# Recurrence's columns ahead of attention's values, and one stream for cached keys and values

## The chip, the cores and the metric

The kernel runs on one core of one Trainium2 chip. The metric is the time on the device of one execution in microseconds (us), the median of three runs. TensorE (PE) multiplies matrices, VectorE (DVE), ScalarE (ACT) and GpSimd (POOL) do the rest, and 16 DMA engines move data between HBM and the on-chip memory. POOL issues the gathers of cached pages, SyncE (SP) all other transfers.

## What is computed

Two decoder layers for a prompt of 256 tokens and 8 samples of one token each, which have 2048 cached positions in pages of 128. All 264 rows go through the same weights. Cut to what matters here, layer 0:

```python
x = x + 0.5 * swiglu(rms_norm(x), w_gate, w_up, w_down)         # FFN 0
qkv, z, b, a, dq, dk, dv = jnp.split(rms_norm(x) @ w_in, ...)   # the mixer's input projection
gq, gk, gv = split(silu(causal_conv(qkv)))                      # the recurrence's queries, keys, values
o_g, S = gdn_chunked(l2norm(gq), l2norm(gk), gv, g, beta, S0)   # samples: gdn_recurrent, one step
o_g = rms_norm(o_g, g_norm) * silu(z)
k, v = gather_pages(cache_diff_k, page_table), gather_pages(cache_diff_v, page_table)   # samples only
o_d = diff_attend(dq, pos, [(k, v, ...), (dk, dv, pos)], lam, ...)   # softmax over the past and the new token
x = x + concat([o_g, o_d]) @ w_out                              # then FFN 1
```

Layer 1 is FFN 2, a latent attention with its own cache (ckv, kpe), and FFN 3; a final norm follows. Everything is float32.

## The kernel before

**Order of work.** The kernel is written as threads (Python generators). A planner, class Clock, estimates when each instruction could start and puts the instructions of all threads into the engines' queues in that order; `urgent` threads have a bonus (gdn and gdn_s 80, proj 0; line 1759), `flow` threads may run ahead. Each queue is then fixed and runs in order on the chip. Where PE would be idle by the plan, it gets matmuls of a constant (tile ps_pe, line 666). Nearly every instruction is issued through line 457, so rows are told apart by their tiles.

**Weights.** Class Stream loads units of 16 blocks of 128 x 128 (1 MB, tile raw), splits them by fours into a high and a low part (ACT and DVE, tile whl), and each block makes three matmuls of 264 columns. `W.limit` stops it at the end of the input projection until post_g calls `W.resume`.

**The mixer of layer 0** (from line 1143). proj (1162) computes the columns of WIN (line 118), 128 features each, eight blocks a column: dq, dk, dv (attention's queries, keys, values), gk, gq, gv (the recurrence's; each goes through a convolution on DVE, ACT and POOL), z. At gk0 it waits for the scores of sample 1 (1169), since tile S2, where the recurrence's columns go, serves as three key slots before. The other threads: dpv (1582) makes the samples' query weights and, after dv3, the token-major values ("vtok"); diff_p (1617) the prompt's attention, after vtok; diff_s (1659) the samples' scores, one sample after the other, by scores (1023); diff_v (1680) weighs their values, by weigh (1057), after vtok; gdn (1266) the recurrence over the prompt, after gk3, gq3 and, in its second half, gv3; gdn_s (1457) its step for the samples, after the last column; post_g (1716) and post_d (1730) the norms and the two halves of the output projection (tile mix).

**The caches.** Class Loader (970) gathers tiles in order into whichever slots are free; a slot is given back when its tile has been used, but not a slot that is a piece of another tile (ya, yb, S2). LK loads keys: per sample 8 tiles of 128 x 1024 (0.5 MB). LV loads values: per sample 4 tiles of 128 x 2048 (1 MB), one for each strip. LK has 4 pieces of ya and yb, 8 own slots (N_DK) and 3 pieces of S2; LV has 2 slots (N_DV). FFN 0 hands them out one by one (`side`). After proj LK gets four whl slots, which it must give back before post_g ("dk retired"); after gdn_s LV gets xh and xl. PE_ has two pairs of score buffers, so scores of sample b wait until sample b - 2 is weighed (1671). Layer 1 has loaders mk (8 slots of 0.65 MB) and mv.

```python
LK = Loader("dk", 1024, [(kpool, ptk[:, i, 4 * b + g:4 * b + g + 1]) for b in range(NS) for i in range(2) for g in range(4)], [])
LV = Loader("dv", 2048, [(vpool, pt[:, 4 * (NS + b) + g:4 * (NS + b) + g + 1]) for b in range(NS) for g in range(4)], [])
```

Of the kernel before, what the change touches and what calls it, by code (L numbers as in the profile page):

```python
# [37 lines left out]
N_DK, N_DV = 8, 2  # L38
N_MK, N_MV = 8, 2
# [78 lines left out]
WIN = [n + str(h) for n in ("dq", "dk", "dv", "gk", "gq", "gv", "z") for h in range(4)]  # L118
# [24 lines left out]
class Virtual:  # L143
    """A tile whose place is chosen when its first instruction is put into a queue."""
# [5 lines left out]
class Slots:  # L150
    """Places of one shape for virtual tiles. The place of a tile is free again when its thread has gone past the
    segment that made it (keep: when the thread has called free) and its last instruction is in a queue."""
# [35 lines left out]
class Clock:  # L188
    """Puts the instructions that the threads create into the engine queues in the order of their
    estimated starts, so that no queue waits long at its head."""  # L190
# [16 lines left out]
    # -- tiles  # L207
# [48 lines left out]
    def when(self, r, write, eng=None):  # L256
        """When an instruction of `eng` may use the region."""
# [32 lines left out]
    # -- cost estimates  # L290
# [47 lines left out]
    # -- instructions  # L338
# [91 lines left out]
    def pe(self, t, c, cols, share):  # L430
        """The tensor engine's clock is halved in each tick after one in which few columns left the array."""
        if self.columns.get(int(t // self.TICK) - 1, 0.0) < self.FULL:
            c *= 2.0
        k = int((t + c) // self.TICK)
        self.columns[k] = self.columns.get(k, 0.0) + cols * share
        return t + c

    def keep_warm(self, t):
        """Matmuls that nobody reads, up to time t."""
# [52 lines left out]
    def add(self, name):  # L492
        """What the current thread has created so far makes `name` available."""
        if not self.cur:
            self.done[name] = 0.0
        else:
            self.cur.marks.append((name, self.seq))
            self.settle(self.cur)

    # -- threads: generators that yield None (go on when all that they issued is done), a time, or the  # L500
    # names they wait for
# [53 lines left out]
def hybrid_trunk_kernel(ctx: ExitStack, tc: tile.TileContext, wall, xT, wba, vecs, cst0, cst1, ident_d, convst,  # L555
# [29 lines left out]
    def service(thread, f, *a):  # L585
        """f's instructions in a thread of their own, which nobody waits for as a whole."""
# [5 lines left out]
    # ------------------------------------------------------------ weight stream  # L592
    class Stream:
        """The weights, 128 x 128 blocks in the order of their use; units of 16 blocks are loaded, pieces of 4 split into
        a high and a low part, except those that raw() hands out whole."""
# [54 lines left out]
        def whole(self, use):  # L650
            """use(the next block); with float32 products for these there is nothing to split."""
# [13 lines left out]
    # in the tensor engine's gaps it multiplies a constant, so that its clock stays up  # L665
# [17 lines left out]
    def rsqrt(src, w, np_=128):  # L683
        """1/sqrt of a small tile on the vector engine."""
# [17 lines left out]
    # ------------------------------------------------------------ constants  # L702
# [30 lines left out]
    # ------------------------------------------------------------ norm statistics  # L733
# [19 lines left out]
    def norm_rows(n, squares, scale, eps):  # L753
        """squares: n tiles [128, NT]. For tile i, rows 32 i and 32 i + 1 of the result add up to
        1 / sqrt(scale * (sum over the partitions) + eps)."""
# [32 lines left out]
    class Rstd:  # L788
        """The thread that computes mul / sqrt(scale * sum of acc over the partitions + eps), for every row; get()
        yields it to a thread that needs it."""  # L790
# [31 lines left out]
    # ------------------------------------------------------------ driver  # L822
    def run(*threads):
        loaders = [LK.thread, LV.thread]
# [5 lines left out]
    def flow(gen, bonus=0.0):  # L830
        """A thread that goes on as soon as its matrix products are in the queue."""
        return gen, True, bonus

    def urgent(gen, bonus=BONUS):
        """A thread whose instructions go first even if others could start a little earlier."""
# [8 lines left out]
    def lead(xh, xl, tags):  # L844
        """The first blocks of a projection; the last rows of x come latest, so the first two blocks alternate."""
# [17 lines left out]
    # ------------------------------------------------------------ FFN  # L863
# [58 lines left out]
    # ------------------------------------------------------------ final norm  # L922
# [18 lines left out]
    def finish_y():  # L941
        """The statistics with the tokens on the partitions; a product with their diagonal spreads them."""
# [21 lines left out]
    # ------------------------------------------------------------ KV gather  # L964
# [3 lines left out]
    ptk = sb.tile([128, 2, 4 * NS], I32, name="ptk")  # L968

    class Loader:  # L970
        """Gathers tiles of 32-row strips of four pages each, in order, into whichever slots are free."""
# [40 lines left out]
        def retire(self, tags):  # L1012
            """These slots are not filled again."""
# [8 lines left out]
    # ------------------------------------------------------------ one sample's softmax over its past  # L1022
    def scores(b, w, load, parts, SM, ready, cc, P, pT):
        """w [128, sub, 32]: the queries, one diagonal block for each page of a strip; parts: for each part
        of the features, its four strips' tiles. Leaves exponentials (strip, page, query row; key) in P,
        transposed in pT; returns the inverses of their sums."""
# [25 lines left out]
        r = small("tr", 1)  # L1052
# [1161 lines left out]
```

## Time and profile before

| | before |
|---|---|
| median of 3 runs | 1344.3 us (1342.5 to 1350.9) |
| span of the profiled execution, first to last instruction | 1297.2 us |
| median less span: what lies around it | 47.1 us |
| PE busy | 1274.9 us, 98% |
| PE weight load, DVE, ACT, POOL busy | 88%, 67%, 45%, 33% |
| DMA | 287.7 MB, mean 222 GB/s |
| mean granted clock of PE | 0.979 of 2.4 GHz |

The profile gives the span of the one execution that it records; its time outside the span isn't shown, so the median stands for the whole. Times in the rows are us from the span's start unless marked ns. Matmuls are pipelined: 282 ns is the length of one of 264 columns, but the next one starts 122 ns later, so durations of single matmuls don't add up; the length of a run of them does. A float32 matmul of attention or recurrence shows as two records. The granted clock is 1.0 at 2.4 GHz and 0.5 at 1.2 GHz.

### The profile page before, as it was taken

Reading aid. Unit: us, or ns where it says so; the run is one execution under the profiler, and the core shown is the slowest. Engines: PE = TensorE matmul, PEld = TensorE weight load, DVE = VectorE, ACT = ScalarE, POOL = GpSimd, SP = SyncE. Lnnn points to the kernel's source line nnn. Section 1 sums busy time; section 2 is a strip of 40 time slices with the busy share of each in tenths; the row PEclk is TensorE's granted clock in tenths of the full one; section 3 lists DMA queues with packets and bytes.
Section 4 is the critical chain, followed back from the end, with each engine's and each line's share of the span. In section 5 each row is a group of like instructions: output and inputs, shape, how many; then the busy total and the mean of one; then the engine's idle time right before and its main releaser. Section 6 shows DMA issues by size and latency. Waiting matters only on the chain.

```text
span 1297.2 us, 28444 instructions
## 1 busy us (share of the span) xinstructions
PE 1274.9 (98%) x11569; PEld 1146.7 (88%) x11569; DVE 874.0 (67%) x1855; ACT 580.7 (45%) x1185; POOL 433.4 (33%) x526
## 2 busy tenths in 40 slices
PE   9999999999999999999999999999999999999997
PEld 7999999967676567999999999999876679999996
DVE  6777667687762767877766777766874449777652
ACT  5555544345411024555554555544432235555541
POOL 3643222355552412553422222212334523322221
PEclk9999999999996879999999999999999999999999
DMA  7776556898897563676755454555467955555551
GB/s 286 264 272 233 192 168 229 285 342 320 304 344 288 167 229 133 230 282 221 260 167 192 163 194 168 191 171 187 161 240 278 393 166 176 191 181 178 195 167 63
DMA packets 52163, 287.72 MB, mean 222 GB/s; under 512 B 6192, under 2 KB 6768, under 8 KB 27200
## 3 DMA queue, kind: packets, MB, share of 16 engines
q1 hardware_dynamic: 28912, 180.77, 40.0%
q0 software_dynamic: 23120, 105.13, 22.3%
q8 instruction: 91, 1.49, 0.4%
q14 instruction: 40, 0.33, 0.1%
HBM read 280.95 MB, written 5.03 MB: 220 GB/s over the span
## 4 chain that ended last, share of the span: by engine, by line
PE 86%; DVE 5%; DMA 3%; issue 2%; ACT 1%; POOL 1%; SPq 0%; POOLq 0%; ACTq 0%; DVEq 0%
PE ps_pd L457 40%; PE ps_pa L457 37%; PE ps_pc L457 5%; PE ps_po L457 3%; DVE whl L457 2%; PE ps_pe L666 2%; DMA dv<-in_vpool_dram,pt 2%; DMA raw<-in_wall_dram 1%; ACT whl L457 0%; DVE wxl L457 0%; DMA x<-in_xT_dram 0%; DVE QW L457 0%; DVE x L457 0%; POOL t L457 0%; DVE QR L457 0%
## 5 line engine op out<-in xcount | busy, mean ns | idle before, releaser
L457 DVE TENSOR_TENSOR whl<-raw,whl 128x512 fp32r<-128x512 f32 x642 | 486.0, 766 | 214.7 <-ACT whl L457 208.3
L457 ACT ACTIVATE whl<-raw 128x512 fp32r<-128x512 f32 x642 | 399.8, 630 | 371.9 <-PE ps_pa L457 195.9
L457 PE MATMUL ps_pa<-wxh,whl 128*128 128x264 f32 x1616 | 325.0, 286 | 1.8 <-ACT t L457 0.8
L457 PEld LDWEIGHTS ps_pa<-wxh,whl 128*128 128x128 f32 x1616 | 260.8, 188 | 11.0 <-issue 6.6
L457 PE MATMUL ps_pd<-wxh,whl 128*128 128x264 f32 x1152 | 233.9, 285 | 0.0
L457 PE MATMUL ps_pa<-wxl,whl 128*128 128x264 f32 x808 | 231.1, 286 | 0.0
L457 PEld LDWEIGHTS ps_pd<-wxh,whl 128*128 128x128 f32 x1152 | 187.6, 188 | 0.9 <-DVE whl L457 0.4
L457 POOL TENSOR_TENSOR t<-t,t 128x264 f32<-128x264 f32 (+1 forms) x100 | 83.1, 831 | 275.6 <-DVE t L457 275.4
L457 PE MATMUL ps_pd<-wxl,whl 128*128 128x264 f32 x576 | 164.1, 285 | 0.0
L457 PEld LDWEIGHTS ps_pa<-wxl,whl 128*128 128x128 f32 x808 | 151.8, 188 | 4.9 <-issue 4.5
L457 PE MATMUL ps_pd<-ah,whl 128*128 128x264 f32 x704 | 130.9, 284 | 0.0
L457 PE MATMUL ps_pa<-ah,whl 128*128 128x264 f32 x704 | 130.7, 284 | 0.0
L457 PEld LDWEIGHTS ps_pd<-ah,whl 128*128 128x128 f32 x704 | 110.0, 188 | 0.0
L457 PEld LDWEIGHTS ps_pa<-ah,whl 128*128 128x128 f32 x704 | 109.9, 188 | 0.0
L457 PEld LDWEIGHTS ps_pd<-wxl,whl 128*128 128x128 f32 x576 | 108.2, 188 | 0.8 <-issue 0.8
L457 PE MATMUL ps_pd<-al,whl 128*128 128x264 f32 x352 | 99.9, 284 | 0.0
L457 PE MATMUL ps_pa<-al,whl 128*128 128x264 f32 x352 | 99.7, 283 | 0.0
L457 POOL TENSOR_TENSOR al<-t,ah 128x264 fp32r<-128x264 f32 x88 | 76.9, 874 | 58.0 <-ACT ah L457 57.9
L457 POOL TENSOR_TENSOR t<-x 128x264 f32<-128x264 f32 x45 | 32.8, 730 | 189.0 <-DVE x L457 183.3
L457 POOL DMA_INDIRECT dk<-in_kpool_dram,ptk x57 | 58.8, 1031 | 56.9 <-PE ps_pc L457 45.2
L457 PE MATMUL ps_pd<-wya,whl 128*128 128x264 f32 x352 | 71.2, 284 | 0.0
L457 PE MATMUL ps_pa<-wya,whl 128*128 128x264 f32 x352 | 71.0, 284 | 0.0
(414 smaller groups left out, 1964.6 us busy)
## 6 DMA issues: line engine op xcount, KB each, us to landing
raw<-in_wall_dram SPq DMA_DIRECT2D x162, 1024.0 KB, 4.9
out_y_dram<-wya SPq DMA_DIRECT2D x4, 264.0 KB, 2.6
xh<-in_rec_dram SPq DMA_DIRECT2D x4, 256.0 KB, 9.5
xl<-in_rec_dram SPq DMA_DIRECT2D x4, 256.0 KB, 17.6
out_recs_dram<-xh SPq DMA_DIRECT2D x4, 256.0 KB, 7.1
out_recs_dram<-xl SPq DMA_DIRECT2D x4, 256.0 KB, 4.3
dk<-in_kpool_dram,ptk POOLq DMA_INDIRECT x57, 6.3
cst<-in_cst_dram SPq DMA_DIRECT2D x1, 838.5 KB, 8.7
```

The costliest lines, as they stand in the source:

```text
L457: f(*a, **k)
L666: clk.spare = lambda: nc.tensor.matmul(pe[0:32, 0:256], busy[:, 0:32], busy, start=True, stop=True)
```

## The change

- WIN: the recurrence's keys and queries (gk, gq) come before attention's values (dv); gv and z stay last. proj's wait at gk0 is gone, S2 is a tile of its own and no slot.
- LK and LV are one Loader of 0.5 MB tiles. A strip of values is two tiles. The order: keys of samples 0 to 3 (LEAD), then values of sample b and keys of sample b + 4 in turn, then the last values. 14 own slots (N_KV) and the four pieces of ya and yb; FFN 0 hands out 18 in its columns 1 to 18. After gdn_s, four pieces of xh and xl.
- Four pairs of score buffers: scores of sample b wait for the weighing of sample b - 4.
- Layer 1: ten key slots (N_MK).
- `dynamic_dma_scratch_size` is 4096 (its default stood before), which frees on-chip memory for the slots.
- Index arithmetic for twice as many value tiles (ptk). Comments are removed too.

```diff
-N_DK, N_DV = 8, 2
-N_MK, N_MV = 8, 2
+N_KV = 14
+LEAD = 4
+N_MK, N_MV = 10, 2
+SCRATCH = 4096
...
-WIN = [n + str(h) for n in ("dq", "dk", "dv", "gk", "gq", "gv", "z") for h in range(4)]
+WIN = [n + str(h) for n in ("dq", "dk", "gk", "gq", "dv", "gv", "z") for h in range(4)]
...
 def weigh(o, pT, load, strips, vs, dv):
-        for v, n in enumerate(strips):
-            yield from load.wait(n)
+        for v, tiles in enumerate(strips):
+            per = 4 // len(tiles)
+            yield from load.wait(*tiles)
...
-                    mm(o[32 * j:32 * j + 8, 0:dv], pT[:, 32 * j + 8 * v:32 * j + 8 * v + 8], load.tiles[n][:, j * dv:(j + 1) * dv],
+                    mm(o[32 * j:32 * j + 8, 0:dv], pT[:, 32 * j + 8 * v:32 * j + 8 * v + 8],
+                       load.tiles[tiles[j // per]][:, j % per * dv:(j % per + 1) * dv],
                        start=v == 0, stop=v == 3, tile_position=(0, 32 * j))
-            load.release(n)
+            load.release(*tiles)
...
+    index, KT, VT_ = [], {}, {}
+
+    def keys(b):
+        KT[b] = [range(len(index) + i, len(index) + i + 4) for i in (0, 4)]
+        index.extend((kpool, ptk[:, i, 4 * b + g:4 * b + g + 1]) for i in range(2) for g in range(4))
+
+    def values(b):
+        VT_[b] = [range(len(index) + i, len(index) + i + 2) for i in (0, 2, 4, 6)]
+        index.extend((vpool, ptk[:, i, 4 * (NS + b) + g:4 * (NS + b) + g + 1]) for g in range(4) for i in range(2))
+
+    for b in range(LEAD):
+        keys(b)
+    for b in range(NS):
+        values(b)
+        if b + LEAD < NS:
+            keys(b + LEAD)
+    LK = LV = Loader("kv", 1024, index, [])
...
-    for i in range(N_DK):
-        side[5 + i] = lambda i=i: LK.add([(kv0, f"dk{i}", [128, 1024])])
-    for i in range(N_DV):
-        side[15 + 3 * i] = lambda i=i: LV.add([(kv0, f"dv{i}", [128, 2048])])
+    for i in range(N_KV):
+        side[5 + i] = lambda i=i: LK.add([(kv0, f"kv{i}", [128, 1024])])
...
-            LK.add(extra(mp, "S2", 1024, 12))
-            S2 = Q0 = K0 = V0 = None
+            S2 = mp.tile([128, 12, NT], F32, name="S2")
+            Q0, K0, V0 = S2[:, 0:4, :], S2[:, 4:8, :], S2[:, 8:12, :]
...
-                    if name == "gk0":
-                        yield from wait(("dsc", 1))
-                        nonlocal S2, Q0, K0, V0
-                        S2 = mp.tile([128, 12, NT], F32, tag="S2", name="S2")
...
-                LV.add([(sb, t, [128, KD, NT]) for t in ("xh", "xl")])
+                LK.add(extra(sb, "xh", 1024) + extra(sb, "xl", 1024))
...
-                    P, pT = PE_[b % 2]
-                    if b > 1:
-                        yield from wait(("dpv", b - 2))
+                    P, pT = PE_[b % LEAD]
+                    if b >= LEAD:
+                        yield from wait(("dpv", b - LEAD))
...
-                yield from wait("gdnp", "gdns", "proj", "dk retired")
+                yield from wait("gdnp", "gdns", "proj", "kv retired")
...
-        "vpool": inp["cache_diff_v"].reshape(npool * 32, 2048),
+        "vpool": inp["cache_diff_v"].reshape(npool * 64, 1024),
...
-    nc = _bacc.Bacc("TRN2", target_bir_lowering=False, num_devices=1)
+    nc = _bacc.Bacc("TRN2", target_bir_lowering=False, num_devices=1, dynamic_dma_scratch_size=SCRATCH)
```

## Rows read from the trace of the kernel before

**Rows 1.** The page: span, busy time of each engine, granted clock in 40 slices

```profile
span 1297.2 us, 28444 instructions
PE 1274.9 (98%) x11569; PEld 1146.7 (88%) x11569; DVE 874.0 (67%) x1855; ACT 580.7 (45%) x1185; POOL 433.4 (33%) x526
PEclk9999999999996879999999999999999999999999
```

**Rows 2.** Busy time by stretch, with granted clock, DMA share and GB/s

```profile
core 0: us, PE busy (x) PEld busy (x) DVE busy (x) ACT busy (x) POOL busy (x), PEclk, DMA share, GB/s
...
240.00:400.00 160.00, 156.15 (x1990) 116.72 (x1988) 115.72 (x326) 59.25 (x152) 77.45 (x111) 1.00 0.90 333
400.00:480.00 80.00, 79.71 (x594) 47.89 (x595) 38.48 (x105) 11.36 (x31) 21.93 (x23) 0.72 0.55 189
480.00:521.00 41.00, 40.02 (x316) 30.96 (x314) 34.29 (x87) 16.88 (x35) 11.14 (x14) 1.00 0.46 171
...
960.00:1040.00 80.00, 78.11 (x1029) 53.36 (x1030) 38.73 (x136) 26.96 (x93) 40.42 (x43) 0.98 0.88 334
```

**Rows 3.** The same for the spare matmuls alone (tile ps_pe): busy, count, clock, DMA

```profile
205.00:386.00 181.00, 6.61 (x48) 1.00 0.86 309
386.00:521.00 135.00, 16.66 (x106) 0.84 0.57 207
```

**Rows 4.** The chain that ended last, in order of time: start us, us, what

```profile
381.87 9.30 DMA dv<-in_vpool_dram,pt
...
407.13 9.82 PE ps_pd L457 x32
```

**Rows 5.** PE's timeline: start us, length of the run, out<-in, records

```profile
226.82 1.96 PE L457 MATMUL ps_pc<-dk,QW 128*32 128x128 f32 x64
...
257.03 1.90 PE L457 MATMUL ps_po<-dv,PT 128*8 128x512 f32 x16
...
329.45 2.25 PE L666 MATMUL ps_pe<-busy 128*32 128x256 bf16 x19
...
495.82 9.82 PE L457 MATMUL ps_pa<-mix,whl 128*128 128x264 f32 x79
```

**Rows 6.** PE's timeline: two pairs of the recurrence's products, full clock

```profile
397.38 0.43 PE L457 MATMUL ps_pd<-yb 64*64 64x128 f32 x2
397.74 0.43 PE L457 MATMUL ps_pd<-yb,ya 64*128 64x64 f32 x2
```

**Rows 7.** POOL's timeline: convolution columns gk0, gq3 and gv3, two key gathers

```profile
251.10 0.12 POOL L457 MEMSET t<- 128x3 f32 x1
...
322.61 0.18 POOL L457 COPY CP<-t 128x11 f32<-128x11 f32 x1
...
358.31 0.66 POOL L457 COPY CP<-t 128x11 f32<-128x11 f32 x1
...
373.17 0.94 POOL L457 DMA_INDIRECT dk<-in_kpool_dram,ptk  x1 [0.30 <-issue]
374.41 0.94 POOL L457 DMA_INDIRECT dk<-in_kpool_dram,ptk  x1 [0.30 <-issue]
```

**Rows 8.** Gathers by tile: landing of keys, then gathers (ns) and landing of values

```profile
DMA to landing us min/median/max: 4.5/6.3/13.9
...
L457 POOL DMA_INDIRECT dv<-in_vpool_dram,pt x32: 933/942/1308, 104.6 to 480.5; - x32
DMA to landing us min/median/max: 5.9/9.5/12.4
```

**Rows 9.** PE's timeline: last value strip, transpose of attention's result, FFN 1's first matmul

```profile
493.21 1.04 PE L457 MATMUL ps_po<-dv,PT 128*8 128x512 f32 x8
...
505.48 0.27 PE L457 MATMUL ps_pd<-ident,AO 128*128 128x128 f32 x1
...
520.67 0.36 PE L457 MATMUL ps_pa<-wxh,whl 128*128 128x264 f32 x1 [0.23 <-DVE x L457]
```

**Rows 10.** Layer 1's gathers, a stretch of 20 us as in rows 2

```profile
1020.00:1040.00 20.00, 19.64 (x275) 13.14 (x274) 8.41 (x27) 5.30 (x18) 9.24 (x10) 1.00 0.94 368
```

## What the change does to the time: the prediction

> **What bounds the kernel now.** I read the page's busy times first, then the clock line, then tables by stage, then the chain of waits, then the timelines of PE and POOL. PE is 98% busy over a span of 1297.2 us, and the other engines are far from it [rows 1]. The reader should see two things that the 98% hides. The spare matmuls that fill gaps count as busy, and so does a matmul at half clock: the clock line falls in three of 40 slices, and in 400 to 480 us the mean grant is 0.72 of 2.4 GHz [rows 1, 2]. Both lie in layer 0's mixer. It begins at about 205 us and ends where the next FFN's first matmul starts, at 520.7 us [rows 9].
>
> What PE wastes in these 316 us:
> Spare matmuls: 48 before 386 us and 106 after [rows 3]; back to back one takes 0.11 us (19 in 2.25 us, the last one's latency off [rows 5]), so 5 + 12 = 17 us.
> Half clock: 80 us at 0.72 [rows 2], so 80 x 0.28 = 22 us.
> That leaves about 277 us of work at full clock. 34 of the 39 wasted us lie after 386 us, when projection is over and PE has only the recurrence's small products and the last samples' attention. No change of order can bring the stage's end before 520.7 - 39 = 482 us by much (the short idle gaps hide a few us more).
>
> DMA bounds the middle: in 240 to 400 us its engines are 0.90 busy at 333 GB/s, afterwards only 0.55 and 0.46 [rows 2]. The chain of waits runs through a value tile's transfer of 9.3 us there, then through the recurrence's products, 32 in 9.8 us [rows 4]. So the stage has a middle bound by the stream and an end in which neither PE nor the stream is used.
>
> **Part by part.**
> *Order of projection.* A column of WIN is 24 matmuls; 79 such matmuls take 9.82 us, so 0.122 each and 2.93 us a column [rows 5]. Keys and queries of the recurrence move up four columns (11.7 us each), attention's values go back eight (23.4 us). But the recurrence gains more, since everything that waits for the values (their weighing, the prompt's attention) no longer stands before it. Today the first such column puts its memset at 251.1 us and the last query column its copy at 322.6 us: 71 us for eight columns [rows 7]. After: 16 columns (47 us), three samples' scores (64 records take 1.96 us, so 3.9 us a sample [rows 5], with the small products about 4.5), the 24 matmuls of the gates (2.9 us) and some 4 us of norms: 205 + 67 = 272 us, 50 us sooner. The last convolution column, whose copy stands at 358.3 us [rows 7], has 24 columns, four samples' scores, the gates and then part of the values' work before it: 205 + 70 + 18 + 3 + 12 (norms, Gram products) + 15 = 323 us, 35 us sooner. The recurrence's second half hangs on it.
>
> *The removed wait* of gk0 for sample 1's scores is worth nothing: that column began as soon as the values' columns were done.
>
> *Attention's values.* Today the first strip is weighed at 257.0 us [rows 5]. After: 20 columns (58.6), four samples' scores (18), gates (3), both norms and the recurrence's head (10), transposes (6), and 3 for gaps: 205 + 99 = 304 us. This is the price of the change, 47 us.
>
> *The stream.* Its bytes don't change: 64 key tiles and, now, 64 value tiles of 0.524 MB. 18 are preloaded (9.4 MB; before 12 of keys and two 1 MB ones of values, 8.4 MB). Before the first weighing the stream can hold four samples of keys (32 tiles) and 14 slots: 46. The other 82 are 43 MB, and beside them run 12.6 MB (columns gv and z 4.2, output projection 4.2, recurrent states in and out 4.2): 56 MB. At the middle's 333 GB/s [rows 2] that is 168 us; at the 368 GB/s of layer 1 [rows 10], 152 us. From 304 us the last value lands at 456 to 472 us; today its last strip is weighed at 493.2 us [rows 9]. What feeds this is the end: keys are through four samples early, so 14 slots hold values alone, where today two do.
>
> *After the last value.* Today 12.3 us pass from that strip to the transpose of the result, with one half of the output projection in the queue before it, then 15.2 us to the next FFN [rows 9]. 79 matmuls of that half take 9.8 of the 12.3 us [rows 5]; they can now be done earlier. So 2.5 to 12.3 us, plus 15.2: 18 to 27 us, and the stream puts the next FFN at 474 to 499 us, middle 487.
>
> *PE's side.* If half of the 39 us of waste stays, the stage ends at 501 us; if none, at 482. The middle, 491, and the stream's 487 must both be met, and they disturb each other: I take 493 us, a gain of 28 us.
>
> *POOL.* Values need 32 more gathers; two stand 1.24 us apart [rows 7], so 40 us more of POOL. POOL is busy 77 of 160 us in the middle and 33 of 121 behind it [rows 2], so this fits. If a gather waits at the head of POOL's queue for a slot, the convolution's adds and the samples' recurrence stand behind it, and for these waits the next head.
>
> *The smaller descriptor space* (4096 where the default was) pays for the slots. The trace doesn't show what it does to a gather. Bounds: nothing, or every gather as long as the 1.31 us of the longest value gather [rows 8] instead of 0.94: 110 x 0.37 = 41 us of POOL's time, which still fits. I take nothing.
>
> *Layer 1*: ten key slots for eight. In 960 to 1040 us DMA is 0.88 busy at 334 GB/s [rows 2]; 2 x 0.655 MB are 3.9 us. Below, nothing, if PE is the limit there; I take 3, nearer to the DMA row.
>
> *At nothing*: the index arithmetic (two short DVE operations in FFN 0, which DVE at 67% hides), more score buffers and their memsets (POOL, before the first sample), the same count of matmuls in weigh. Uncovered they would be under 1 us.
>
> Sum: 28 + 3 = 31 us. The page's span is 1297.2 us, the median of the runs 1344.3; I carry the 47.1 us around the span unchanged: 1313 us, a span of 1266.
>
> **A rule that speaks against it.** In the trace a key tile of half the size lands in 6.3 us, a value tile in 9.5 [rows 8]; taken in turn, two halves would cost 3.1 us more, but they aren't taken in turn: with tiles of 0.5 and 0.65 MB alone layer 1 moves 368 GB/s [rows 10]. By the Trainium skill (DMA: Bandwidth & Descriptors, "Anatomy of one DMA" and "Measured") a gather costs some 2.0 us fixed plus its bytes, and one should batch to 1 MiB or more; by that, an estimate from the page, 32 extra gathers would cost 64 us where they don't overlap. The 368 GB/s speak against it as long as several are in flight.
>
> **The rivals.**
> *A, the end stays as it is.* The recurrence's small products run without dense matmuls beside them wherever they stand: today a pair takes 0.36 us at full clock [rows 6] but 32 products take 9.82 us, 0.61 a pair, at half [rows 4]. If they only move forward and the waste goes with them, the stage keeps its 316 us, give or take 8. For it: projection ends sooner too, so nothing dense is left beside them. Against: value strips arrive more densely then, and 14 slots let them be weighed in any gap. Time: layer 1's 3 us alone, 1344 - 3 = 1341 us.
> *B, values start too late.* The recurrence's threads have a bonus of 80 in the planner, projection none. If values' columns go at the pace of today's eight columns (71 us, 8.9 each [rows 7]), the twelve columns from gk0 on take 107 us from 239 us, and the first weighing is at 352 us. Each us of this is one of the end: 352 + 160 + 23 = 535 us, 14 later than today, 1344 + 14 - 3 = 1355 us, or 352 + 168 + 27 = 547 us and 1367 with the slow ends. It decides from 338 us on (338 + 183 = 521). For it: 14 slots full of tiles that nobody may use yet, and a stream that stands still: 28 tiles after the preloaded ones and some 6 MB of weights are 21 MB, 62 us at 333 GB/s, from the first scores at 227 us [rows 5] to about 290. Against: what slowed those columns was largely the values' and the prompt's own attention, which now waits behind them.
> *C, half-size tiles cost their fixed part.* 32 x 3.1 us by rows, if gathers ran in turn, against the 31 gained: up to 1344 + 68 = 1412 us. Only likely if the stream runs with one or two gathers in flight; with 14 slots I give it little.
> *D, everything fits*: stage end at 477 us, the short gaps filled too, and layer 1's 4 us: 1344 - 44 - 4 = 1296 us.
>
> **Numbers.** Faster or slower by 1% is about what a measurement here can tell from no change (13 us). Forecast, with its own range of 1299 to 1330 us: 0.58. D: 0.07. A: 0.21. B: 0.11. C: 0.03. Faster 0.58 + 0.07 = 0.65; same 0.21; slower 0.14. Eight in ten: from D's edge, 1293, to 1350, which takes in A and leaves out B, C and little below.
>
> **What would show it.** Right: the last query column's copy near 272 us, the first value weighed near 304, the last near 460 to 475, the next FFN near 493, fewer than 154 spare matmuls and a grant above 0.72 behind projection, DMA above 0.8 from 304 to 440 us. Wrong: a first weighing after 338 us (B), the recurrence's pairs still at 0.61 us and the stage as long as before (A), gathers of 1.3 us or a stream under 330 GB/s with slots free (C or the descriptor space).

## The result and the profile after

| | before | after |
|---|---|---|
| median, the pair of the result | 1346.4 us (1342.5 to 1350.9, 4 runs) | 1364.2 us (1363.4 to 1368.3, 4 runs) |
| median, both on a chip of the faster level | 1299.0 us (10 runs) | 1308.5 us (7 runs) |

The change makes the kernel slower by 1.4%: the ratio is 1.0138, 95% interval 1.0109 to 1.0167. The same kernel, with the same instructions, takes about 1298 us on two of the chips that the runs name and about 1347 us on two others, called the faster and the slower level below. By its span (1297.2 us) the profile ahead of the prediction is of the faster level, by their length (1342.5 to 1350.9 us) the times beside it are of the slower one. The page of after is of the slower level too, so it can't be laid beside [rows 1] as it stands. On a chip of the faster level the change costs 0.7%: ratio 1.0070, interval 1.0043 to 1.0097.

The page of after (slower level): span, busy time, granted clock in 40 slices.

```profile
span 1366.5 us, 28658 instructions
PE 1310.4 (96%) x11638; PEld 1165.4 (85%) x11638; DVE 874.4 (64%) x1855; ACT 580.3 (42%) x1185; POOL 467.0 (34%) x560
PEclk9999999899898589999999999999999999999999
```

From here on, the changed kernel as it ran on the faster level (label e10_after_again), which answers [rows 2, 3, 7, 9] like for like. Its table by stretch, as in [rows 2]:

```profile
240.00:400.00 160.00, 150.17 (x1966) 112.79 (x1968) 108.05 (x307) 56.98 (x147) 90.42 (x124) 1.00 0.82 309
400.00:480.00 80.00, 79.04 (x582) 46.54 (x578) 33.78 (x81) 9.30 (x26) 35.80 (x38) 0.77 0.65 240
480.00:521.00 41.00, 40.20 (x340) 28.90 (x333) 34.55 (x110) 13.43 (x31) 2.66 (x5) 1.00 0.39 131
```

The same for the spare matmuls alone, as in [rows 3]:

```profile
205.00:386.00 181.00, 11.23 (x87) 1.00 0.77 288
386.00:532.00 146.00, 19.25 (x136) 0.87 0.58 208
```

Its timeline, POOL's, SP's and PE's lines (start us, us, engine, what, in brackets the idle time before it and what ended it):

```profile
293.20 0.19 POOL L459 COPY CP<-t 128x11 f32<-128x11 f32 x1
...
317.24 0.99 POOL L459 DMA_INDIRECT kv<-in_kpool_dram,ptk  x1 [22.84 <-PE ps_po L459]
...
327.78 0.74 POOL L459 TENSOR_TENSOR t<-t,t 128x256 f32<-128x256 f32 x1
328.46 0.19 POOL L459 COPY CP<-t 128x11 f32<-128x11 f32 x1
...
368.11 0.20 POOL L459 COPY CP<-t 128x11 f32<-128x11 f32 x1
...
480.01 0.62 POOL L459 DMA_DIRECT2D out_recp_dram<-SS  x1
482.31 2.63 SPq L459 DMA_DIRECT2D out_recs_dram<-xl  x4
...
315.92 1.04 PE L459 MATMUL ps_po<-kv,PT 128*8 128x512 f32 x8
501.03 1.04 PE L459 MATMUL ps_po<-kv,PT 128*8 128x512 f32 x8
532.42 0.36 PE L459 MATMUL ps_pa<-wxh,whl 128*128 128x264 f32 x1 [0.24 <-DVE x L459]
```

The reader is to see: the stage of layer 0's mixer ends at 532.4 us, where it ended at 520.7 [rows 9]. The waste didn't shrink: 223 spare matmuls for 154, a grant of 0.77 for 0.72 in 400 to 480 us, DMA down from 0.90 to 0.82 in the middle. In the prediction's own way of counting that is 25 + 18 = 43 us where it was 39. The last query column is done 29 us sooner than before (293.2 for 322.6 [rows 7]), but the last convolution column, gv3, 10 us later (368.1 for 358.3 [rows 7]).

### The profile page after: what moved, and what is told of

Its sections match the earlier page's. It is cut to its first block, busy times and chain, and to the rows that moved or that the text cites. A ratio compares the mean times of both kernels' runs of the same rounds, so it can differ in the third digit from the quotient of the medians.

```text
span 1366.5 us, 28658 instructions
## 1 busy us (share of the span) xinstructions
PE 1310.4 (96%) x11638; PEld 1165.4 (85%) x11638; DVE 874.4 (64%) x1855; ACT 580.3 (42%) x1185; POOL 467.0 (34%) x560
## 4 chain that ended last, share of the span: by engine, by line
PE 83%; DVE 7%; issue 4%; DMA 2%; another core or an unknown queue 1%; ACT 1%; POOL 1%; POOLq 0%; ACTq 0%; DVEq 0%; SPq 0%
PE ps_pd L459 38%; PE ps_pa L459 34%; PE ps_pc L459 5%; PE ps_po L459 3%; PE ps_pe L668 3%; DVE whl L459 2%; DMA raw<-in_wall_dram 2%; DVE t L459 1%; ACT whl L459 1%; DVE QW L459 0%; POOL t L459 0%; DVE wxl L459 0%; DVE x L459 0%; DVE yb L459 0%
## 5 line engine op out<-in xcount | busy, mean ns | idle before, releaser
L459 DVE TENSOR_TENSOR whl<-raw,whl 128x512 fp32r<-128x512 f32 x642 | 485.9, 766 | 210.7 <-ACT whl L459 204.6
L459 PE MATMUL ps_pa<-wxh,whl 128*128 128x264 f32 x1616 | 329.3, 289 | 4.4 <-issue 2.2
L459 PEld LDWEIGHTS ps_pa<-wxh,whl 128*128 128x128 f32 x1616 | 264.2, 191 | 11.4 <-issue 7.9
L459 PEld LDWEIGHTS ps_pa<-wxl,whl 128*128 128x128 f32 x808 | 154.7, 192 | 6.0 <-issue 5.6
L459 POOL DMA_INDIRECT kv<-in_vpool_dram,ptk x64 | 60.9, 952 | 72.3 <-PE ps_pc L459 45.1
L459 POOL DMA_INDIRECT kv<-in_kpool_dram,ptk x60 | 62.0, 1033 | 68.7 <-PE ps_pc L459 31.6
L459 ACT ACTIVATE t<-t 128x264 f32<-128x264 f32 (+1 forms) x106 | 43.7, 412 | 84.5 <-DVE t L459 61.8
```

Source lines behind the costliest of these rows:

```text
L459: f(*a, **k)
```

## The experiments

One table first, from the traces. "gv3" is the issue of CP's store right after the last convolution column; "first" and "last strip" are the start of the first and the end of the last weighing of values; "recurrence" is the later of two issues, that of the prompt's final state (out_recp, which POOL issues, so SyncE doesn't issue all stores) and the last of the samples' states (out_recs); "FFN 1" is its first matmul, the end of the stage. The last two columns are FFN 1 less recurrence and less last strip. F and S are the faster and the slower level.

| run | level | time us | ratio to before | gv3 | first strip | recurrence | last strip | FFN 1 | less rec. | less strip |
|---|---|---|---|---|---|---|---|---|---|---|
| e1 before | F | 1299.2 | 1.000 | 359.7 | 257.4 | 470.1 | 494.2 | 520.6 | 50.5 | 26.4 |
| e2 space only | F | 1294.0 | 0.996 | 359.5 | 256.9 | 471.3 | 495.3 | 521.7 | 50.5 | 26.4 |
| e3 order only | F | 1346.5 | 1.036 | 354.6 | 320.3 | 484.7 | 549.0 | 569.3 | 84.5 | 20.2 |
| e4 stream, old order | F | 1319.4 | 1.015 | 374.8 | 273.7 | 496.6 | 485.9 | 550.3 | 53.7 | 64.4 |
| e5 after | S | 1366.5 | 1.014 | 392.3 | 328.6 | 533.8 | 552.8 | 583.1 | 49.4 | 30.3 |
| e6 e4, POOL relieved | S | 1376.0 | 1.022 | 401.0 | 283.3 | 539.2 | 517.5 | 583.0 | 43.8 | 65.5 |
| e7 after, POOL relieved | S | 1386.9 | 1.029 | 397.8 | 323.8 | 559.6 | 549.7 | 602.4 | 42.7 | 52.7 |
| e8 before, POOL relieved | S | 1344.5 | 0.999 | 379.9 | 263.0 | 500.3 | 526.1 | 552.9 | 52.7 | 26.9 |
| e10 after | F | 1308.5 | 1.007 | 368.3 | 315.9 | 484.6 | 502.1 | 532.4 | 47.8 | 30.3 |
| e13 after, columns first | F | 1322.9 | 1.018 | 313.5 | 324.4 | 435.9 | 529.4 | 549.6 | 113.7 | 20.2 |
| e14 after, 2 in front | F | 1319.8 | 1.015 | 364.4 | 314.3 | 482.4 | 529.0 | 550.3 | 68.0 | 21.3 |
| e15 old order, 2 in front | F | 1301.0 | 1.003 | 365.2 | 257.2 | 475.8 | 481.9 | 527.3 | 51.5 | 45.3 |
| e16 before, columns first | F | 1315.1 | 1.012 | 343.1 | 249.6 | 469.5 | 518.5 | 538.7 | 69.3 | 20.2 |
| e17 after, gv first | S | 1380.4 | 1.024 | 344.7 | 360.0 | 503.0 | 578.0 | 598.3 | 95.3 | 20.2 |
| e18 e15, gq and gv first | S | 1364.5 | 1.013 | 360.8 | 263.3 | 522.2 | 531.1 | 574.8 | 52.6 | 43.7 |

e9, e11 and e12 are e1, e3 and e4 again, on e10's chip: 1301.9 (one run), 1347.0 and 1320.4 us. A time is compared by its ratio to the kernel before on its own chip, and only within a level, since the ratio of the change itself differs between them (1.007 and 1.014). The rows of the table are one profiled execution each.

### The kernel before, for its own time

No edit.

> The kernel before, unchanged, to see what its own profile and its own time have to do with each other. Theory O (the 47.1 us between the page's span and the median are an overhead around the span): span near 1297 again and time near 1344. Theory M (the profiled execution of before was another one, some 45 us faster than the timed ones): span within 2 us of the time, as with the changed kernel (1366.5 in 1368.31), so a span near 1342 to 1350 and 45 us more somewhere inside it; the stage that ended at 520.7 us would then end later, or FFN and layer 1 would be longer.

> The kernel before once more, for its profile. The times so far fall into two levels by chip: 1298 us on one, 1347 us on the other, with the same instructions. Theory F: on the slower chip PE waits in its dense runs of small matmuls for nothing that the profile shows (issue), as the changed kernel does there (one sample's scores in 8.4 us, where 3.6 on the faster chip). If this chip is of the slower level: span 1340 to 1350 us, scores of samples 2 to 4 in 6 to 9 us each, next FFN near 550 us. If of the faster: 1297 us and 520 us again.

1299.2 us (1296.2 to 1302.9, 10 runs); the profiled execution has a span of 1298.4 and a time of 1300.3. Neither theory held as it was put: nothing lies around the span, and no 45 us lie inside this execution. The 1344 us fit a chip of the slower level; the record names no chip for them. e9 also ran on the faster level, so there is no profile of the unedited kernel on the slower one; e8, which takes the same time there (ratio 0.9988, interval 0.9967 to 1.0010), stands for it. The expectations of e2 to e4 count from 1344 us, so their times have to be moved down by some 47 us before a result is held against them.

### The smaller descriptor space alone

```diff
-    nc = _bacc.Bacc("TRN2", target_bir_lowering=False, num_devices=1)
+    nc = _bacc.Bacc("TRN2", target_bir_lowering=False, num_devices=1, dynamic_dma_scratch_size=4096)
```

> The kernel before with the smaller descriptor space alone (4096), with its slots as they were. Theory R (the descriptor space costs the 20 us): 1355 to 1368 us, gathers longer than 0.94 us or more than 1.24 us apart, or POOL waiting ahead of a gather for nothing that the profile shows. Rival (order and stream cost them): 1342 to 1351 us, as before, gathers of 0.94 us. If the space decides the 47 us outside the span, the span comes within 2 us of the time here and not in the unchanged kernel.

Ratio 0.9963, interval 0.9936 to 0.9989: not a cost but a small gain, the only edit whose interval lies below 1. The mixer of layer 0 is as it was (521.7 for 520.6). From FFN 1 to the end it takes 772.1 us for 777.8 (e9: 775.3). All profiles of the faster level agree: 771.8 to 773.1 us with the smaller space (e2, e4, e10, e12 to e15), 775.3 to 777.8 without (before, e1, e3, e9, e11, e16). The loads of weights (tile raw) place it: the 126th of 165 is issued 421.6 us behind FFN 1 in e2 and 421.5 in e1, the 138th 583.5 and 588.1, so it arises in the stretch that holds layer 1's attention. Why is not shown.

### The two halves of the change, and both

```diff
-WIN = [n + str(h) for n in ("dq", "dk", "dv", "gk", "gq", "gv", "z") for h in range(4)]
+WIN = [n + str(h) for n in ("dq", "dk", "gk", "gq", "dv", "gv", "z") for h in range(4)]
```

This line alone in the kernel before is e3; taken back in the changed kernel it gives e4.

> The kernel before with the new order of the columns alone (keys and queries of the recurrence ahead of attention's values; two loaders, two pairs of score buffers and the wait of gk0 for sample 1's scores stay). Theory V (values come late, and the stream stands still until they do): first value strip weighed after 300 us, only 10 slots to bridge it with, so slower than before: 1360 to 1385 us. Rival S (the single stream with four samples of keys in front is what costs): 1335 to 1350 us, with the recurrence's scan starting some 40 us sooner.

> The changed kernel with the old order of the columns (attention's values ahead of the recurrence's), all else as changed. Theory V: the first value strip is weighed near 260 us, the stream doesn't stand still for 44 us, and the time falls by 20 us or more, to 1345 us or below. Rival S (single stream, four samples of keys in front): the values' slots stay full of keys, POOL's head waits for a slot as before, and the time stays at 1355 to 1368 us.

> The changed kernel, unchanged, beside the kernel before on the same chip. In the runs so far the kernel before took 1298.5 us where the pair shown for the prediction has 1346. Order alone cost 48 us there, the single stream alone 21. Theory Sum (the two costs add): 1360 to 1372 us, ratio 1.05. Theory One chain (both delay the same end): 1345 to 1352 us, ratio 1.04. Either way its profile has the first value strip weighed near 329 us and the next FFN near 583 us.

> The changed kernel again, beside the two halves of the change. On a chip of the slower level: 1364 to 1368 us, ratio 1.014. On one of the faster level, Theory Sum: 1298 + 48 + 21 = 1360 to 1372 us; Theory One chain: 1345 to 1352 us; Theory F (what the changed kernel loses on the slower chip it loses to issue): 1310 to 1335 us.

> The new order of columns alone, beside the whole change on the same chip. On a chip of the faster level 1346 us as before. On one of the slower level, Theory V (the values come late, and their stream ends the stage whatever PE's pace): 1347 + 35 to 50 = 1382 to 1397 us. Rival: what the order costs is hidden behind PE's slower pace there, 1350 to 1365 us.

> The single stream with the old order of columns, on the same chip. On a chip of the faster level 1319 us as before. On one of the slower level, Theory P (POOL's gathers hold the recurrence back): 1360 to 1370 us, as much as the whole change, so that the new order costs nothing on top of it. Rival: 1345 us or below, and then the new order is all of the 19 us.

On the faster level the order alone costs 48 us, the single stream alone 21 (e4 has the smaller space, the buffers and the slots of layer 1 as well), both together 9.5. So the halves don't add (Theory Sum fell), and neither does the larger one set the price (One chain fell too): each makes good for part of the other's harm. e5 came to lie on the slower level, so e10 answers for it: 1308.5 us, just below its own Theory F's 1310 to 1335. e3's 1346.5 us lies in rival S's range only because that range counts from 1344; 48 us above its own kernel before is Theory V. e4's Theory V fell: taking the old order back makes the changed kernel slower, 1319.4 us for e10's 1308.5. e11 and e12 ran on the faster level and repeat e3 and e4; what was expected of the slower one stays untested. PE's timeline of e3, the first and the last strip and FFN 1, and before them POOL's last gather ahead of the first strip and the next one:

```profile
248.88 0.94 POOL L457 DMA_INDIRECT dk<-in_kpool_dram,ptk  x1 [0.30 <-issue]
...
321.68 0.99 POOL L457 DMA_INDIRECT dv<-in_vpool_dram,pt  x1 [3.94 <-PE ps_po L457]
...
320.32 1.90 PE L457 MATMUL ps_po<-dv,PT 128*8 128x512 f32 x16
...
547.99 1.04 PE L457 MATMUL ps_po<-dv,PT 128*8 128x512 f32 x8
...
569.25 0.37 PE L457 MATMUL ps_pa<-wxh,whl 128*128 128x264 f32 x1 [0.23 <-DVE x L457]
```

With the order alone the first strip waits until 320 us, and the last is weighed 55 us later than before; FFN 1 follows 20.2 us behind it. That is rival B's mechanism: the stream stands still with its slots full, no gather is issued from 249 to 321 us. In e4 it is the other way round: the last strip is weighed 8 us sooner than before, yet the stage ends 30 us later, 54 us behind the recurrence.

### Is it POOL's head?

```diff
-                        G.tensor_tensor(y[:, 0:NP], y[:, 0:NP], t[:, 0:NP], OP.add)
+                        V.tensor_tensor(y[:, 0:NP], y[:, 0:NP], t[:, 0:NP], OP.add)
...
-                G.memset(SS, 0.0)
+                V.memset(SS, 0.0)
```

and likewise the convolution's memset, other add and copy, and the memsets of bt and of the samples' operands.

> The changed kernel with the old order of columns, and the recurrence's small POOL instructions (the four of each convolution column, and the memsets of bt, SS and the samples' operands) on DVE, so that none of them stands behind a gather. Theory P (the single stream's 64 + 64 half-size gathers hold POOL's head and delay the recurrence): SS's memset before 412 us where it was 436.3, the next FFN near 520 us where it was 550, and the time falls from 1319 to 1285 to 1300 us. Rival (the recurrence is late for PE or DVE, not for POOL): 1312 to 1325 us, since DVE gets some 1.4 us more for each of twelve columns.

> The changed kernel with the same instructions on DVE, new order kept. Theory P: the copy of column gv3 falls from 392 to 350 us, SS's memset from 468 to 430 us; but the values then set the end alone (first strip weighed at 329, last at 552), so the next FFN falls only to 560 to 575 us and the time by 8 to 20 us. Rival Order (values come late whatever POOL does, and the recurrence isn't what ends the stage): no more than 5 us. Third: if the value gathers are what waits for POOL, both ends move and the time falls by 30 us or more.

> The kernel before with the same instructions on DVE. Its POOL waited 78 us at gathers' heads in the mixer and its memset of the samples' operands (389.5 us) came right behind eleven gathers in a row. Theory P, if it holds here too: 1285 to 1293 us. Rival (two loaders of fewer, larger tiles leave POOL free enough, and the values set the end): 1295 to 1303 us.

Theory P fell. The prediction's fear came true in form: the timeline above has a gather that waits 22.84 us at POOL's head for a slot, and gv0's larger add comes only at 327.78, behind eight gathers. But without these instructions on POOL gv3 isn't earlier (e7 397.8 for e5's 392.3), and the changed kernel is 20 us slower still. The plan is made anew with such an edit and puts the samples' recurrence later (state stored at 559.6 for 533.8), and DVE has more to do, so these runs speak against POOL's head as what holds gv3 back; they don't price the wait itself. A count on the faster level agrees with them: of the chain of waits in e10 from 293 to 420 us, gathers on POOL are 2.7%, 3.4 us. e8 behaves as its rival says (ratio 0.9988). e6 ran on the slower level and can't be laid beside e4.

### What ends the stage

```diff
-            run(..., dpv(), flow(proj(), 0.0), post_g())
+            run(..., dpv(), flow(proj(), 80.0), post_g())
```

in the changed kernel (e13) and in the kernel before (e16); in e17 the bonus begins at gv0.

> The changed kernel, with a bonus of 80 in the planner for the projection's thread (0 before), so that its columns are no longer put behind weighings, scores and the prompt's attention. The copy of column gv3 should come at 320 to 340 us instead of 368 (392 on the slower chip). Theory T (the stage ends some 164 us after gv3): next FFN at 485 to 505 us where it was 532, and the time falls by 25 us or more, to 1285 us or below (1340 or below on the slower chip). Theory V (values end the stage): the weighing comes no earlier, the next FFN stays at 525 to 540 us, the time within 8 us of 1308.5 (1366).

> The kernel before with the same bonus for the projection's columns. Theory T: gv3's copy at 320 to 335 us instead of 358, next FFN at 490 to 505 us, time 1270 to 1285 us on the faster chip. Theory V: the values, which the columns now push back, end the stage as late or later: 1297 to 1320 us.

> The changed kernel, in which the projection's thread has its bonus of 80 from column gv0 on only, so that no weighing and no scores stand between the values' columns and gv3. Theory Two ends (the next FFN at the later of gv3 + 162 us and the last strip + 21 us): gv3's copy at 325 to 340 us instead of 368, so the recurrence would allow 487 to 502 us; but the first strip is weighed 10 to 18 us later and the last one at 505 to 520, next FFN 526 to 541, time within 10 us of 1308.5 on the faster chip (1366 on the slower). Rival T (the recurrence alone): next FFN at 487 to 502 us, time 1265 to 1280.

The timeline of e13, POOL's and PE's lines: gv3's copy, the final state, the last strip, FFN 1.

```profile
313.33 0.19 POOL L459 COPY CP<-t 128x11 f32<-128x11 f32 x1
435.92 0.60 POOL L459 DMA_DIRECT2D out_recp_dram<-SS  x1 [0.52 <-DVE t L459]
...
528.77 0.60 PE L459 MATMUL ps_po<-kv,PT 128*8 128x512 f32 x2
...
549.59 0.36 PE L459 MATMUL ps_pa<-wxh,whl 128*128 128x264 f32 x1 [0.23 <-DVE x L459]
```

With the columns first, gv3 is done at 313, ten us earlier than the prediction wanted it, and the recurrence ends 49 us sooner than in e10. The stage still ends 17 us later, 20.2 us behind the last strip. Theory T (the recurrence alone) fell. The values decide, as Theory V says, but later than it allowed (FFN 1 at 549.6 us for 525 to 540), since the columns push the weighings back. e16 is the same on the kernel before: Theory V's range held (1315.1 us). The table's last two columns show what stands in its place: FFN 1 comes about 43 to 54 us behind the recurrence or 20 to 21 us behind the last strip, whichever is later. The code agrees: post_g starts when both parts of the recurrence are done, and the second half of the output projection waits for the first half and for the last sample's values. In six runs (e3, e13, e14, e16, e17 and the repeat e11) the strip decides, at 20.2 or 21.3 us; in the others the recurrence. The timeline of e1, where the recurrence decides:

```profile
470.11 0.60 POOL L457 DMA_DIRECT2D out_recp_dram<-SS  x1 [5.99 <-DVE SS L457]
...
493.15 1.04 PE L457 MATMUL ps_po<-dv,PT 128*8 128x512 f32 x8
...
520.60 0.37 PE L457 MATMUL ps_pa<-wxh,whl 128*128 128x264 f32 x1 [0.23 <-DVE x L457]
```

The strips would have allowed 494.2 + 20.2 = 514.4 us there. So the kernel before had 6 us of room behind its values, no more, and the values and the recurrence compete for PE. The expectation's fixed distance behind gv3 is none: from gv3 to the recurrence's end it is 110 us in e1 and 116 in e10, but 122 in e13 and 126 in e16, and on the slower level 158 in e17 for 142 in e5, since what the columns overtake then lies behind them. e17 has the direction of Theory Two ends and not its sizes: the first strip came 31 us later than in e5, not 10 to 18, the last at 578 us, and the time was 1380.4 us, 14 above 1366, not within 10.

### How many samples of keys in front

```diff
-LEAD = 4
+LEAD = 2
```

in the changed kernel (e14), and with the old order of columns (e15); e18 is e15 with the bonus from gq0 on.

> The changed kernel with keys of two samples in front instead of four (and two pairs of score buffers), new order of columns kept. Theory L (four samples of keys are what bridges the time until values may be used): the stream stands still from sample 1's scores to the first weighing with its slots full of values, and the time goes to 1340 to 1355 us on the faster chip, near the order alone (1346). Rival (the slots, not the keys in front, make the difference): 1300 to 1315 us.

> The single stream with the old order of columns and keys of two samples in front. Theory L: with values usable at 260 us, keys of four samples in front only delay the values and the first weighing (273.7 where it was 257.4); with two the 21 us are given back: 1290 to 1302 us on the faster chip. Rival (the single stream costs by its half-size tiles and its one queue): 1315 to 1325 us as with four.

> The single stream with the old order, keys of two samples in front (1301 us on the faster chip) and the projection's bonus of 80 from column gq0 on. There the recurrence ended the stage (gv3 at 365 us, 162 later 527) and the last strip, weighed at 481 us, left 25 us of room. Theory Two ends: gv3 at 342 to 355 us, last strip at 488 to 500, next FFN at 507 to 521 us, time 1280 to 1295 us, below both kernels. Rival (with half-size tiles the stage keeps its length whatever comes first): 1298 to 1310 us.

With the new order, two samples in front cost 11 us against four: the last strip is weighed at 529 for 502. Theory L had the direction and the standstill (no gather is issued from 259 to 316 us, in e10 from 277 to 317), not the size: 1319.8 us lies nearer to its rival's range. The rest of the way from 1346 us (order alone) to 1320 lies with the single stream and its 14 slots for either kind, and some 5 us with the descriptor space; these were not taken apart. With the old order it is the reverse, and Theory L held: two samples in front give back 18 of the 21 us. The timeline of e15:

```profile
475.78 0.62 POOL L459 DMA_DIRECT2D out_recp_dram<-SS  x1 [11.34 <-DVE t L459]
...
480.88 1.04 PE L459 MATMUL ps_po<-kv,PT 128*8 128x512 f32 x8
...
527.25 0.36 PE L459 MATMUL ps_pa<-wxh,whl 128*128 128x264 f32 x1 [0.23 <-DVE x L459]
```

Here the values are through 12 us sooner than before, the one thing that the prediction promised of the stream, and it buys nothing, since the recurrence ends 6 us later and FFN 1 follows it by 51.5. e18 tried to use that room, but ran on the slower level, where neither of its ranges applies: 1364.5 us, 1.3% above the kernel before. Its scan begins (SS's memset) 108 us behind gv3, where it is 76 in e5 on the same level, so gv3 at 361 us brought no earlier end.

## Why the prediction was wrong

The rows of the prediction are of the faster level, so its steps are held against e10.

**The base.** The 47.1 us "around the span" don't exist: time less span is 1.7 to 3.1 us in every execution that shows both. The sum was a difference, so this spoiled the absolute number and not the sign.

**The step that failed: what ends the stage.** The sum let two bounds end it, the last value plus 18 to 27 us (487 us in the middle) and PE's waste halved (491). Neither held: the last strip is weighed at 502.1 us where the value was to land at 456 to 472, and the waste is 43 us for 39. By the 20.2 us that lie behind the values alone, the strips allow no FFN 1 before 522.3 us, later than the 520.7 of before; so this term alone takes the whole gain away. And the end that did decide, the recurrence's at 484.6 us plus 47.8, was no term of the sum. It stood there only as gv3, "35 us sooner"; gv3 came 10 us later than before. e13 and e15 show that either end by itself is enough to hold the stage: in e13 gv3 is early and the strips decide (549.6 us), in e15 the strips are early and the recurrence decides (527.3 us). The reading behind it, a middle bound by the stream, was thin: of the chain of waits in the 316 us of before, transfers of values are 21 us; in e10 no such transfer is left in the stage's chain, and the stage is 12 us longer.

**gv3 at 323 us.** It came at 368. Of the 45 us, 21 were lost by the last query column (below) and 24 behind it: from that column's copy to gv3's the sum had 51 us, 15 of them for "part of the values' work", and it measures 75 (293.2 to 368.1). With the columns and norms as summed (23 and 8 us), and with the fourth sample's scores, which the sum had here, already done, that term is about 43 us. PE's list for 294 to 368 us in e10 (matmuls by form, count, busy us, mean ns):

```profile
L459 PE MATMUL ps_pa<-wxh,whl 128*128 128x264 f32 x117 | 24.2, 296 | 0.0
L459 PE MATMUL ps_pa<-wxl,whl 128*128 128x264 f32 x59 | 17.3, 293 | 0.0
L459 PE MATMUL ps_po<-kv,PT 128*8 128x512 f32 x88 | 11.3, 594 | 0.0
L459 PE MATMUL ps_pc<-kv,QW 128*32 128x128 f32 x256 | 10.3, 279 | 0.0
```

176 matmuls of columns are 7.3 columns; at 2.93 us they are 21.5 us of the 74. The rest are norms and what the values' columns set free: 11 strips weighed (88 records at 8 a strip), the fifth and sixth sample's scores (256 records at 128 a sample) and, in groups not shown, the prompt's attention and the recurrence's first half. In WIN the values' columns now stand between the recurrence's queries and gv, so all of this stands there too. e17 shows it from the other side: with gv ahead of the weighings, gv3 comes 48 us sooner than in e5 on the same level.

**The last query column**: 272 forecast, 293.2 measured. The direction was right. 9 of the 21 us are a price too low: the four gq columns stand at 281.2, 285.5, 289.4 and 293.2, 4.0 us apart, not 2.93, and there are eight. 9 more are the fourth sample's scores, which the sum had behind this column: they run at 261.4 to 270.4 us, with waits for keys that were gathered only as slots came free (the third's take 3.7).

**The first value weighed**: 304 forecast, 315.9 measured (328.6 to 329.4 on the slower level). Rival B's threshold of 338 wasn't reached.

**The last value**: 456 to 472 forecast, 502.1 measured. The bytes per us weren't the error: in 328 to 368 us the stream runs at 372 GB/s, 0.97 of the DMA engines. Later it waits for slots. They become free when PE scores or weighs what is in them, and PE's queue holds the last sample's scores (405 to 436 us) and the weighings (436 to 447, 458 to 468 and 476 to 485 us) between the steps of the scan. POOL's timeline of e10 has the longest of these later waits:

```profile
436.55 0.94 POOL L459 DMA_INDIRECT kv<-in_vpool_dram,ptk  x1 [16.46 <-PE ps_pc L459]
```

The prediction counted the stream and PE's waste as two bounds that disturb each other by 2 us; in fact scores and weighings are part of the same queue as the scan.

**After the last value**: this was misread in the kernel before. [rows 9] has 27.5 us from the start of the last strip to FFN 1 (26.4 from its end), and the prediction took them for the price of the values' end, 9.8 of which could move. The first half of the output projection waited for the recurrence (470.1 + 50.5 = 520.6); behind the values alone lie 20.2 us. So both ends had to be moved, the recurrence's first, and the change moved both the wrong way.

**POOL**: the extra gathers fit, as said; the wait at its head came, 22.84 us, and nothing points to it as what held gv3.

**The descriptor space**, taken at nothing, is worth about 5 us, behind FFN 1. **Layer 1**: from FFN 1 to the end e10 takes 771.8 us, the kernel before 775.3 to 777.8. That is the sign of the forecast 3 us and about its size, but by luck: e2, with eight key slots, already has 772.1. The two further slots show nothing.

**The page's rule** (Trainium skill, DMA: Bandwidth & Descriptors, "Anatomy of one DMA") would have made 32 extra gathers cost 64 us, an estimate from it, where they don't overlap. The trace doesn't bear that out here: with the old order and two samples in front the half-size stream costs 3.5 us (interval 1.4 to 6.0) together with the gain of the descriptor space, so some 8 without it, by estimate.

**The rivals.** A comes nearest to the result on the faster level: the waste stays, and the stage keeps nearly its length (316 us then, 327 now, 3 more than A's give or take 8). It didn't stay for A's reason, a scan that only moves forward: the scan begins later (SS's memset at 419.5 us in e10, 410.8 before). B's mechanism is what the order does alone (e3), and it is there in the whole change in part: no gather is issued from 277 to 317 us in e10, where B had the stream stand still from about 290 to 352. C and the slow gathers have no support.

**The slower level** adds the rest. From e8, which stands for before, to e5 the stage there goes from 552.9 to 583.1 us, 30 longer, where it is 12 on the faster level. What differs is seen below; its cause stays open.

Not tried: post_g's wait for "kv retired", which now takes in values' tiles in the borrowed slots. In e10 the first half's first matmul, at 499.6 us, stands ahead of the last strip, and 15 us behind the samples' last state (22 in e4), so nothing pointed to it.

## What to carry to other kernels

Before moving work, find every chain that meets at the stage's end and give each its own distance to that end, from runs in which it is the last; the room between them is all that one of them can bring. An order of work and the buffers that bridge it are one choice: here four samples in front suit the new order and two the old one, and with four in front either half alone is worse than both. Look whether the profiled execution's span and the timed runs agree to within a few us before anything is summed; if not, they may not be of one chip.

## What the runs showed of the hardware

The same instructions take 1298 us on two chips and 1347 on two others. On the slower ones PE pauses in its dense runs of small matmuls for nothing that the profile shows. It isn't so from the start: the second sample's scores take 3.7 us on both levels (e5: 241.9 to 245.6 us). The third sample's scores, 128 records, in the changed kernel, PE's timeline; first e10 on the faster level:

```profile
252.66 3.70 PE L459 MATMUL ps_pc<-kv,QW 128*32 128x128 f32 x128
```

and e5 on the slower level:

```profile
254.83 1.52 PE L459 MATMUL ps_pc<-kv,QW 128*32 128x128 f32 x39
256.66 2.29 PE L459 MATMUL ps_pc<-kv,QW 128*32 128x128 f32 x56 [0.30 <-issue]
259.25 0.43 PE L459 MATMUL ps_pc<-kv,QW 128*32 128x128 f32 x6 [0.30 <-issue]
259.98 0.44 PE L459 MATMUL ps_pc<-kv,QW 128*32 128x128 f32 x5 [0.30 <-issue]
260.70 0.45 PE L459 MATMUL ps_pc<-kv,QW 128*32 128x128 f32 x6 [0.29 <-issue]
```

3.7 us become 8.7, at a granted clock of 0.98. From 250 to 520 us PE's gaps that end in nothing but "issue" are 16.6 us in e5 and 15.2 in e8, on the faster level 0.6 in e10 and none in e1. In 240 to 400 us PE is busy 140.65 us there, where it is 150.17 on the faster level, and the granted clock is 0.93 where it is 1.00 (e5's row by stretch):

```profile
240.00:400.00 160.00, 140.65 (x1463) 102.29 (x1461) 91.40 (x268) 53.91 (x137) 76.85 (x112) 0.93 0.74 260
```

Packets of 4096 bytes take 159 ns at the median on both levels, so the DMA engines don't show it. What PE waits for in these pauses, and why the clock is lower there, is not settled by these runs.
